# One query tile turned two k-steps later, an output projection that begins with its high parts, and late splits of the second half, in a two-layer decoder step

## The chip, the cores and the metric

The kernel runs on one core of a Trainium2 chip. The metric is the device time of one execution in microseconds (us), the median of several runs; lower is better. The core has a matrix engine (PE; its weight loads are listed apart, as PEld), a vector engine (DVE), a scalar engine (ACT), a general engine (POOL) and a synchronising engine (SP) that here mostly issues transfers (DMAs).

## The reference

One inference step of a decoder with two layers. Layer 0 is a state-space mixer (Mamba-2) and a SwiGLU feed-forward; its output gives one shared set of keys and values. Layer 1 is sliding-window attention with grouped heads over those keys and values, then its output projection, then a second SwiGLU; a final RMS norm ends it. 1024 prompt tokens with 16 learned tokens ahead of them, and 8 x 8 sampled tokens, go through the same weights. The change touches layer 1's attention alone, whose core is

```python
hn = _rmsnorm(h, p['attn_norm_g'][i])
q = _rope_partial((hn @ p['w_q'][i]).reshape(b, l, N_HEADS, HEAD_DIM), pos)
mix = _sliding_sink_attention(q, k_all, v_all, pos0, p['attn_sinks'][i]) @ p['w_o'][i]
h = h + mix
```

All of it is float32, with 16 query heads of 64, 4 key/value heads, and 1024 model columns.

## The kernel before, in words

Activations lie with the model columns on the 128 partitions (8 slices, the k-steps) and the tokens along the free dimension, in two halves of 544 columns in the stage looked at here. A float32 product is made of three products of rounded parts, high by high, high by low and low by high (`mm3`, L75 to L78). The high part of an operand is an ACT cast and the low part a DVE subtraction that waits for the cast (`split_copy`, L81 to L83, for activations; `factor`, L1259 to L1265, for weights: L1263 on ACT, L1264 on DVE).

**Queries.** The generator `queries` (L2237) goes over a = 0 and 1 (the first and the second eight heads) and over prompt tiles i = 1 to 8: eight k-steps of `mm3` give a tile of 128 tokens by 512 query columns. At the last k-step `put_q` scales it on ACT (L2192) and rotates it on POOL (four L2007, then L2008 and L2009) into a tile `qr`. The tile waits in the list `turned`, and during the next tile's k-steps, at k = 5, `turn_queries` transposes it on PE (L2234, four of 128x128) and DVE copies it to QT (L2235). So there are 16 such turns, the last one by itself at the end. For the second heads the weights are split anew: ACT casts (L2028) and DVE subtractions (L2029).

**Attention.** Between these steps `mix` puts the steps of 16 units (`PromptUnit`: tile i, heads a): scores on PE (L2303) with mask and maximum on DVE (L2309), softmax (DVE L2318, L2319, L2327, L2328; ACT exponentials L2326; POOL L2329), and two units later the transposes of the weights (PE L2342, ACT copy L2344, DVE copy L2349) and the values (PE L2360, L2364; copies L2367) into u.O. The last two units run beside the output projection.

**Output projection.** `split` casts and subtracts a unit's u.O into OH[e] and OL[e], the parts of half e (units of tiles 1 to 4 belong to half 0, of tiles 5 to 8 to half 1; a = 0 fills k-steps 0 to 3 and a = 1 fills 4 to 7); the sampled tokens fill the first 32 columns (`split_sampled`). `output_early` (L2472) then makes half 0: for each m of 8 column slices, and each of two chunks c of 272 columns, 24 matmuls into one PSUM tile, the sum with the residual on DVE (L2488), its square on ACT (L2465), and at c = 1 a store to memory that ACT issues (L2491). It yields after every second k-step, and `mix(att, early, 2, 5)` puts steps of the last two units there. `output_tile` (L2496) makes half 1 with k outermost (48 matmuls per m), beside `scale_early`, which turns the squares of half 0 into the norm's scale (PE L1190, DVE L1195 and L1196, POOL L92, DVE L1210, PE L1211, ACT L1212) and applies it to half 0 as loaded back from memory (DVE L1414, L1408, L1415).

**What sets the order.** PE's order here is the program's (`in_order`, L1113); the other engines' is a scheduler's, with priorities (`tc.high_priority`). SP loads, in its own order, each m's slice of w_o in four pieces of 128 KB (L2605) into a ring `ws` of six, the residual rows (L2479), and back from memory the halves hN1 and hN0, two slices m at a time (L2645). The factors `wo` lie in a ring of 12, which is three m.

Of the kernel before, what the change touches and what calls it, by code (L numbers as in the profile page):

```python
# [21 lines left out]
KD = 8  # L22
# [33 lines left out]
EARLY = 14  # L56
# [18 lines left out]
def mm3(nc, out, wH, wL, xH, xL, start, stop):  # L75
    nc.tensor.matmul(out, wH, xH, start=start, stop=False)  # L76
    nc.tensor.matmul(out, wH, xL, start=False, stop=False)  # L77
    nc.tensor.matmul(out, wL, xH, start=False, stop=stop)  # L78


def split_copy(nc, H, L, src):  # L81
    nc.scalar.copy(H, src)
    nc.vector.tensor_tensor(L, src, H.bitcast(F32), ALU.subtract)  # L83
# [1029 lines left out]
def in_order(tc, instructions, engine):  # L1113

    last = None
    for i in instructions:
        if i.engine == engine.engine:
            if last is not None:
                info = mybir.DependencyInfo(mybir.DependencyClass.NoSync, mybir.DependencyReason.DATA)
                tc.add_manual_dep(i, last.name, info, reason="order")  # L1120
            last = i
# [24 lines left out]
def together(a, b):  # L1146

    for _ in a:
        next(b, END)
        yield  # L1150
    for _ in b:
        pass
# [115 lines left out]
class Units:  # L1268
# [22 lines left out]
    def rows(self, w0, w1):  # L1291


        def load(t, w):
            self.nc.sync.dma_start(t[:], w)

        def blocks(r0, r1):
            return {"A11": r0[:, :512], "A21": r0[:, 512:], "A12": r1[:, :512], "A22": r1[:, 512:]}

        self.queue.append([load, (w0, w1), blocks, None])  # L1300
# [824 lines left out]
def qkv(tc, K, A, ap, fp, ps, O, I, pre):  # L2125


    nc = tc.nc
    cs = lambda i, n: A.rope[:n, 8 * i : 8 * i + 8]
    sn = lambda i, n: A.rope[:n, 72 + 8 * i : 80 + 8 * i]  # L2130
    size = lambda i: 128 if i else NX
    start = lambda i: NX + 128 * (i - 1) if i else 0
# [12 lines left out]
    def rows_mm(i, w):  # L2145

        n = size(i)
        acc = ps.rows()
        for k in range(KD):
            mm3(nc, acc[:n, :], *pre.operand(k, i), w[k][0][:], w[k][1][:], k == 0, k == KD - 1)  # L2150
            yield acc
# [36 lines left out]
    def put_q(i, acc, dst):  # L2188
        n = dst.shape[0]
        v = lambda t, p: t.rearrange(p, e=2, q=4)  # L2190
        for e in range(2):
            nc.scalar.mul(v(dst, "p (q e d) -> p e q d")[:, e], v(acc[:n, :], "p (e q d) -> p e q d")[:, e], r8[i][:n])  # L2192
        rope_rows(nc, fp, dst, n, 8, cs(i, n), sn(i, n), nc.gpsimd)

    late = []
# [14 lines left out]
    with tc.high_priority(PRIO):  # L2210
        w = [pre.weights.split(k, raw[0][k], K.g_attn) for k in range(KD)]
# [17 lines left out]
    def turn_queries(i, a, rows):  # L2229

        pq = ps.turned()
        pv = pq[:].rearrange("p (j s h c) -> p j h s c", j=2, s=2, h=2)
        for q in range(4):
            nc.tensor.transpose(pv[:, q // 2, q % 2], rows[:, 128 * q : 128 * q + 128], K.ident)  # L2234
        nc.vector.tensor_copy(A.QT[:, i - 1, a], pq[:])  # L2235

    def queries(w):  # L2237
        turned = [sampled_turned]
        for a in range(2):
            for i in range(1, 9):  # L2240
                for k, acc in enumerate(rows_mm(i, w)):
                    if k == 5 and turned:
                        turned.pop(0)()
                    if k == KD - 1:
                        dst = fp.tile([128, 512], F32, name="qr", tag="row", bufs=2)[:]
                        put_q(i, acc, dst)
                        turned.append(lambda i=i, a=a, dst=dst: turn_queries(i, a, dst))
                    if k % 2:
                        yield
            if a == 0:  # L2250
                with tc.high_priority(PRIO):
                    w = [pre.weights.split(k, raw[1][k], K.g_attn) for k in range(KD)]
        A.last_turn = turned.pop(0)

    return queries(w)


# [202 lines left out]
def output_square(nc, K, F, sqh, hv, e, m, o=0):  # L2460

    n = hv.shape[1]
    d = K.tot[:, 544 * e + o : 544 * e + o + n]
    t = d if m == 0 else sqh()[:, :n]
    nc.scalar.activation(t, hv, AF.Square)  # L2465
    if m == KD - 1 and e:
        F.last_square = t
    elif m:
        (nc.vector if e or m == KD - 1 else nc.gpsimd).tensor_tensor(d, d, t, ALU.add)


def output_early(nc, K, F, sqh, rows, oH, oL):  # L2472


    for m in range(KD):
        u = F.units.get(1)
        w = [u.factor(nm) for nm in ("lo", "hi")]
        x = F.units.raw()[:, :544]
        nc.sync.dma_start(x, F.saved[0][:, m])  # L2479
        F.units.load(2)  # L2480
        for c in range(2):
            acc = rows()
            cs = slice(272 * c, 272 * c + 272)
            for k in range(KD):
                wH, wL = (t[:, 128 * (k % 4) : 128 * (k % 4) + 128] for t in w[k // 4])
                mm3(nc, acc[:, :272], wH, wL, oH[:, k, cs], oL[:, k, cs], k == 0, k == KD - 1)
                if k == KD - 1:
                    nc.vector.tensor_tensor(x[:, cs], x[:, cs], acc[:, :272], ALU.add)  # L2488
                    output_square(nc, K, F, sqh, x[:, cs], 0, m, 272 * c)
                    if c:  # L2490
                        nc.scalar.dma_start(F.saved[0][:, m], x)  # L2491
                if k % 2:
                    yield
# [19 lines left out]
def attention(tc, K, I, O, pre):  # L2513


    nc = tc.nc
    A, F = Ctx(), pre.F
    tp = lambda **kw: tc.tile_pool(reuse_waits="tile", **kw)
    traced = nc.cur_bb.bb.instructions
    with ExitStack() as outer:  # L2520
        outer.enter_context(F.stack.pop_all())
        with ExitStack() as inner:
# [32 lines left out]
            with tp(name="qf", bufs=1) as fp:  # L2555
# [9 lines left out]
                units = [PromptUnit(K, A, i, a, sp, ps) for a in range(2) for i in range(8)]  # L2565

                def prompt(first, last, done=lambda u: None):

                    n = len(units)
                    for x in range(first, last):  # L2570
                        if x >= 2:
                            units[x - 2].turn(0)
                        if x < n:
                            units[x].scores(0)
                        yield
                        if x >= 2:
                            units[x - 2].turn(1)
                        if x < n:
                            units[x].scores(1)
                            units[x].softmax()  # L2580
                        yield
                        if x >= 2:
                            units[x - 2].values()
                            done(units[x - 2])
                            yield
# [6 lines left out]
                att = together(prompt(0, EARLY), sample)  # L2592
# [25 lines left out]
            def split(u):  # L2618

                e, fs, o = u.i // 4, slice(4 * u.a, 4 * u.a + 4), 32 + 128 * (u.i % 4)  # L2620
                split_copy(nc, OH[e][:, fs, o : o + 128], OL[e][:, fs, o : o + 128], u.O)

            def split_sampled(e, o, a, b):
                split_copy(nc, OH[e][:, :, o : o + b - a], OL[e][:, :, o : o + b - a], A.OS[:, :, a:b])

            with tc.high_priority(PRIO):
                split_sampled(0, 0, 40, 64)
                split_sampled(0, 24, 32, 40)
                for i in range(4):
                    split(units[i])  # L2630
                    split(units[8 + i])
            split_sampled(1, 0, 0, 32)
            for i in range(4, 8):
                split(units[i])
            early = output_early(nc, K, F, sqh, ps.rows, OH[0], OL[0])
            att = prompt(EARLY, len(units) + 2, split)
            for _ in range(AHEAD):
                next(att)
            A.last_turn()
# [9 lines left out]
        for m in range(KD):  # L2649
            at = len(traced)  # L2650
# [16 lines left out]
def trunk(tc, I, O):  # L2667
    K = Ctx()
    K.nc = tc.nc
    with tc.tile_pool(name="const", bufs=1) as cp:  # L2670
        build_consts(tc, K, cp, I)
        K.cp = cp
        K.h = [cp.tile([128, KD, 592], F32, name="hA", tag="h0")]
        K.tot = cp.tile([128, 1104], F32, name="tot")
        with tc.tile_pool(name="w1", bufs=1) as wp:
            Q = Weights(tc.nc, wp)
            m = Mamba(tc, K, cp, Q, I, O)
            m.run()
        pre = Prepare(tc, K, I)
        m.F.run(pre)  # L2680
        attention(tc, K, I, O, pre)
# [124 lines left out]
```

## Time and profile before

| | us |
|---|---|
| median of 3 runs | 2751.78 |
| lowest and highest | 2743.92, 2752.15 |
| the profiled execution | 2752.1 |
| its span on the core | 2750.3 |
| PE busy in the span | 2690.7 (98%) |
| DVE, ACT, POOL busy | 1937.3, 1180.9, 499.1 |

The span is the time from the first to the last instruction in the trace; all times inside it are counted from its start. The queries and the attention of layer 1 lie at about 1700 to 1940, the early output projection at 1905 to 1971, the second half's at 1971 to 2020. PE is busy nearly all the time, so the stretches in which it stands are what a change of order can win.

### The profile page before, as it was taken

What the parts mean: (1) busy time and instruction counts of PE and PEld (TensorE: products, weight loads), DVE (VectorE), ACT (ScalarE), POOL (GpSimd) and SP (SyncE); (2) the same over time, 40 slices, a digit from 0 to 9 for tenths busy, and PEclk for the clock granted to TensorE, in tenths of its full rate; (3) what the DMA queues carried; (4) which work ended last, traced back from release to release, by engine and by line L of the source; (5) the groups of instructions that cost most, each with busy time, mean ns of one, the idle gap of its engine ahead of it and who ended that gap; (6) DMA issues with size and microseconds to landing.
All of it is one profiled execution on the core that took longest, in us unless ns stands there. A gap on an engine that the chain in (4) does not pass through costs nothing. (4 is left out here: it accounts for less than half of the span.)

```text
span 2750.3 us, 49923 instructions
## 1 busy us (share of the span) xinstructions
PE 2690.7 (98%) x19545; PEld 2491.6 (91%) x19545; DVE 1937.3 (70%) x3354; ACT 1180.9 (43%) x2480; POOL 499.1 (18%) x707
## 2 busy tenths in 40 slices
PE   8999999999999999999999999999999999999998
PEld 7888898987888899999999997676999999999998
DVE  6878666576564787777778881556488777777887
ACT  5766544266441543333342143556344333334123
POOL 3566544025322000000000002433200000000001
PEclk9999999999999999999999999999999999999999
DMA  8876766665554344444487652011724444447764
GB/s 292 281 240 221 261 233 241 235 225 194 191 187 157 111 160 154 146 136 163 145 300 277 228 193 82 27 48 32 214 68 150 160 144 136 159 144 284 273 231 165
DMA packets 266347, 501.00 MB, mean 182 GB/s; under 512 B 23792, under 2 KB 144240, under 8 KB 266112
## 3 DMA queue, kind: packets, MB, share of 16 engines
q1 hardware_dynamic: 262368, 491.10, 52.2%
q10 hardware_dynamic: 3744, 6.72, 0.7%
q8 instruction: 154, 2.52, 0.4%
q14 instruction: 81, 0.66, 0.1%
HBM read 322.44 MB, written 175.30 MB: 181 GB/s over the span
## 5 line engine op out<-in xcount | busy, mean ns | idle before, releaser
L1263 ACT CAST wo<-ws 128x512 fp32r<-128x512 f32 x424 | 261.8, 621 | 493.9 <-PE wacc L1625 218.4
L1625 PE MATMUL dacc<-bo,wo 128*128 128x276 f32 (+1 forms) x1232 | 356.1, 289 | 0.0
L1624 PE MATMUL dacc<-bo,wo 128*128 128x276 f32 (+1 forms) x1232 | 355.0, 288 | 0.0
L1626 PE MATMUL dacc<-bo,wo 128*128 128x276 f32 (+1 forms) x1232 | 354.9, 288 | 0.0
L1264 DVE TENSOR_TENSOR wo<-ws,wo 128x512 fp32r<-128x512 f32 x424 | 290.2, 689 | 50.3 <-ACT wo L1263 46.7
L76 PE MATMUL acc<-uH,wH 128*128 128x336 f32 (+2 forms) x808 | 266.2, 329 | 7.0 <-DVE th L850 5.6
L78 PE MATMUL acc<-uH,wL 128*128 128x336 f32 (+2 forms) x808 | 266.8, 330 | 1.3 <-POOL wL L150 1.2
L77 PE MATMUL acc<-uL,wH 128*128 128x336 f32 (+2 forms) x808 | 265.9, 329 | 0.0
L1624 PEld LDWEIGHTS dacc<-bo,wo 128*128 128x128 f32 x1232 | 232.8, 189 | 0.4 <-ACT sumX L1813 0.4
L1626 PEld LDWEIGHTS dacc<-bo,wo 128*128 128x128 f32 x1232 | 231.8, 188 | 0.0
L1625 PEld LDWEIGHTS dacc<-bo,wo 128*128 128x128 f32 x1232 | 231.8, 188 | 0.0
L76 PEld LDWEIGHTS acc<-uH,wH 128*128 128x128 f32 x808 | 154.0, 191 | 22.0 <-DVE th L850 5.8
L668 DVE SCALAR_TENSOR_TENSOR cc<-raw,vectors_sb,cc 128x616 f32<-128x616 f32 (+1 forms) x144 | 138.5, 966 | 42.2 <-ACT cc L666 40.3
L78 PEld LDWEIGHTS acc<-uH,wL 128*128 128x128 f32 x808 | 153.6, 190 | 13.6 <-issue 3.7
L77 PEld LDWEIGHTS acc<-uL,wH 128*128 128x128 f32 x808 | 153.7, 190 | 11.3 <-issue 2.7
L76 PE MATMUL acc<-yH,wH 128*128 128x336 f32 (+1 forms) x360 | 122.8, 341 | 8.3 <-DVE hA L930 2.6
L2543 POOL MEMSET mask<- 128x64 f32 x1 | 0.2, 152 | 706.1 <-PE dacc L1626 706.1
L78 PE MATMUL acc<-yH,wL 128*128 128x336 f32 (+1 forms) x360 | 120.8, 335 | 0.6 <-DMA wL<-kept 0.6
L77 PE MATMUL acc<-yL,wH 128*128 128x336 f32 (+1 forms) x360 | 120.5, 335 | 0.7 <-DVE yL L83 0.7
L1263 ACT CAST wo<-sum 128x512 fp32r<-128x512 f32 x62 | 38.5, 621 | 174.9 <-PE wacc L1625 130.7
L1624 PE MATMUL wacc<-N4H,wo 128*128 128x276 f32 (+1 forms) x352 | 102.2, 290 | 3.7 <-DVE hN L1644 2.0
L1801 DVE TENSOR_TENSOR hN<-hN,dacc 128x552 f32<-128x552 f32 (+1 forms) x128 | 91.7, 722 | 19.1 <-PE dacc L1626 18.6
(576 smaller groups left out, 8425.0 us busy)
## 6 DMA issues: line engine op xcount, KB each, us to landing
kept<-wH SPq DMA_DIRECT2D x56, 512.0 KB, 2.8
kept<-wL SPq DMA_DIRECT2D x56, 512.0 KB, 3.1
ws<-ffn_w_gate SPq DMA_DIRECT2D x44, 512.0 KB, 4.2
ws<-ffn_w_up SPq DMA_DIRECT2D x44, 512.0 KB, 5.1
ws<-ffn_w_down SPq DMA_DIRECT2D x44, 512.0 KB, 5.9
ws<-ssm_w_in SPq DMA_DIRECT2D x40, 512.0 KB, 5.3
wH<-kept SPq DMA_DIRECT2D x38, 512.0 KB, 3.6
wL<-kept SPq DMA_DIRECT2D x38, 512.0 KB, 4.5
```

What stands on the lines that cost most here:

```text
L76: nc.tensor.matmul(out, wH, xH, start=start, stop=False)
L77: nc.tensor.matmul(out, wH, xL, start=False, stop=False)
L78: nc.tensor.matmul(out, wL, xH, start=False, stop=stop)
L668: nc.vector.scalar_tensor_tensor(o, raw[:, k : k + n], w(k), o, ALU.mult, ALU.add)
L1263: nc.scalar.copy(H, src)
L1264: (low or nc.vector).tensor_tensor(L, src, H.bitcast(F32), ALU.subtract)
L1624: nc.tensor.matmul(out, wH, xH, start=start, stop=False, skip_group_check=True)
L1625: nc.tensor.matmul(out, wH, xL, start=False, stop=False, skip_group_check=True)
L1626: nc.tensor.matmul(out, wL, xH, start=False, stop=stop, skip_group_check=True)
L1801: add = lambda d, s: nc.vector.tensor_tensor(d, d, s, ALU.add)
L2543: nc.gpsimd.memset(A.mask0[:, :NS], NEG)
```

## The change

It has three parts. The turn of the first heads' last tile, which happens during the second heads' first tile, is made at k = 7 and not at k = 5. The first chunk of the output projection makes all its products with OH first (16 matmuls) and then those with OL (8), all before its first yield. The splits of half 0 run in the order of units 0, 1, 8, 9, 2, 3, 10, 11 (before: 0, 8, 1, 9, 2, 10, 3, 11), and those of half 1 are all put behind the values of the last unit, chained in that order on ACT and on DVE.

```diff
-                    if k == 5 and turned:
+                    if k == (KD - 1 if a and i == 1 else 5) and turned:
                         turned.pop(0)()
...
+            if m == 0 and c == 0:
+                for late in range(2):
+                    for k in range(KD):
+                        wH, wL = (t[:, 128 * (k % 4) : 128 * (k % 4) + 128] for t in w[k // 4])
+                        if late:
+                            nc.tensor.matmul(acc[:, :272], wH, oL[:, k, cs], start=False, stop=k == KD - 1)
+                        else:
+                            nc.tensor.matmul(acc[:, :272], wH, oH[:, k, cs], start=k == 0, stop=False)
+                            nc.tensor.matmul(acc[:, :272], wL, oH[:, k, cs], start=False, stop=False)
             for k in range(KD):
-                wH, wL = (t[:, 128 * (k % 4) : 128 * (k % 4) + 128] for t in w[k // 4])
-                mm3(nc, acc[:, :272], wH, wL, oH[:, k, cs], oL[:, k, cs], k == 0, k == KD - 1)
+                if m or c:
+                    wH, wL = (t[:, 128 * (k % 4) : 128 * (k % 4) + 128] for t in w[k // 4])
+                    mm3(nc, acc[:, :272], wH, wL, oH[:, k, cs], oL[:, k, cs], k == 0, k == KD - 1)
...
-                for i in range(4):
-                    split(units[i])
-                    split(units[8 + i])
-            split_sampled(1, 0, 0, 32)
-            for i in range(4, 8):
-                split(units[i])
+                for i in (0, 2):
+                    for a in range(2):
+                        split(units[8 * a + i])
+                        split(units[8 * a + i + 1])
+            def split_later(u):
+                if u is units[-1]:
+                    at = len(traced)
+                    split_sampled(1, 0, 0, 32)
+                    for x in range(4, 8):
+                        split(units[x])
+                        split(units[8 + x])
+                    for eng in (nc.vector, nc.scalar):
+                        last = [i for i in traced[at - 40 : at] if i.engine == eng.engine][-1]
+                        in_order(tc, [last] + traced[at:], eng)
+
-            att = prompt(EARLY, len(units) + 2, split)
+            att = prompt(EARLY, len(units) + 2, split_later)
```

The order of PE around the moved turn, before (-) and now (+); L2342 and L2360 are steps of the attention units, L77 and L78 the query tile's products:

```order
 L77 MATMUL pP<-rwL,u_17269 128x512
 L78 MATMUL pP<-rwH,u_17270 128x512
-L2234 MATMUL pT<-cmask_sb,qr 128x2x64 x4
 L2342 MATMUL pT<-cmask_sb,work 128x128
 L2342 MATMUL pO<-cmask_sb,work 128x128
...
 L77 MATMUL pP<-rwL,u_17269 128x512
 L78 MATMUL pP<-rwH,u_17270 128x512
+L2234 MATMUL pT<-cmask_sb,qr 128x2x64 x4
 L2360 MATMUL pO<-work,V 64x256 x4
 L2364 MATMUL pO<-work,V 64x256 x4
```

One turn, the eighth of 16, has moved behind six more products of its neighbour tile and one step of attention.

The order of DVE from the projection's first subtractions on (OL_20182 is half 0, OL_20183 half 1; L2498 is L2488 of before):

```order
 L83 TENSOR_TENSOR OL_20182<-QT,OH_20180 128x4x128 x6
-L83 TENSOR_TENSOR OL_20183<-OS,OH_20181 128x8x32
-L83 TENSOR_TENSOR OL_20183<-QT,OH_20181 128x4x128 x4
-L1264 TENSOR_TENSOR wo<-ws,wo 128x512
-L2327 TENSOR_TENSOR work<-work 128x4
-L2309 ISA work<-pS,am_sb,sink 128x192
...
+L83 TENSOR_TENSOR OL_20183<-OS,OH_20181 128x8x32
+L2498 TENSOR_TENSOR ws<-ws,pP 128x272
+L83 TENSOR_TENSOR OL_20183<-QT,OH_20181 128x4x128 x5
+L2498 TENSOR_TENSOR ws<-ws,pP 128x272
+L83 TENSOR_TENSOR OL_20183<-QT,OH_20181 128x4x128 x3
+L1264 TENSOR_TENSOR wo<-ws,wo 128x512
```

Five subtractions of half 1 have left the place ahead of the score step L2309, and all nine now stand together after the last unit.

The order of DVE around the scale of half 0, in the second half's projection (hN_21010 is half 0 as loaded back, hN_21011 half 1; L2518 is L2508 of before):

```order
-L2508 TENSOR_TENSOR hN_21011<-hN_21011,wacc 128x544
-L1264 TENSOR_TENSOR wo<-ws,wo 128x512
+L2518 TENSOR_TENSOR hN_21011<-hN_21011,wacc 128x544
 L1414 TENSOR_TENSOR sum<-hN_21010,tot 128x256
 L1408 SCALAR_TENSOR_TENSOR hN_21010<-hN_21010,vectors_sb,tot 128x512 x5
 L1415 TENSOR_TENSOR hN_21010<-sum,vectors_sb 128x8x32
 L1408 SCALAR_TENSOR_TENSOR hN_21010<-hN_21010,vectors_sb,tot 128x512 x3
-L1264 TENSOR_TENSOR wo<-ws,wo 128x512
-L1245 TENSOR_TENSOR sum<-ws 128x512
-L2508 TENSOR_TENSOR hN_21011<-hN_21011,wacc 128x544
+L1264 TENSOR_TENSOR wo<-ws,wo 128x512 x2
+L2518 TENSOR_TENSOR hN_21011<-hN_21011,wacc 128x544
```

A weight's subtraction that stood ahead of the group L1414 to L1408 stands behind it now; it is that of k-steps 4 to 7 of m = 3, made from ws_21054. On SP the pieces of ws_21054 have moved too (before, then now; L2615 is L2605 and L2664 is L2645 of before):

```order
-L2605 DMA ws_21054<-w_o 64x4x128 x3
-L2605 DMA ws_21119<-w_o 64x4x128 x4
-L2645 DMA hN0_21010<-res0_9633 128x2x544
-L2605 DMA ws_21054<-w_o 64x4x128
-L2605 DMA ws_21219<-w_o 64x4x128 x4
...
+L2615 DMA ws_21359<-w_o 64x4x128 x4
 L1284 DMA ws_21364<-ffn_w_gate 128x8x128
-L2645 DMA hN0_21010<-res0_9633 128x2x544
+L2664 DMA hN0_21010<-res0_9633 128x2x544 x2
+L2615 DMA ws_21054<-w_o 64x4x128 x2
```

Two of the four pieces now come after everything else of w_o and after both last loads of hN0.

## Rows read from the trace of the kernel before

**Rows 1.** The list of waits of PE, 1500 to 2100: us, times, longest.

```profile
PE pT L2234 <- POOL qr L2009: 3.7, 2, 2.9
PE pP L77 <- DVE OL L83: 2.2, 1, 2.2
PE ps L1211 <- DVE tot L1210: 1.9, 1, 1.9
```

**Rows 2.** The timeline of PE, the seventh and the eighth turn: start, us, [idle before].

```profile
1784.12 0.66 PE L2234 MATMUL pT<-cmask_sb,qr 128*128 128x128 f32 x4 [2.92 <-POOL qr L2009]
...
1799.97 0.60 PE L2234 MATMUL pT<-cmask_sb,qr 128*128 128x128 f32 x4
```

**Rows 3.** The timeline of POOL, the rotations of those two tiles.

```profile
1778.85 4.55 POOL L2007 TENSOR_TENSOR rt<-qr,rope_sb 128x64 f32<-128x64 f32 x4
...
1792.86 1.14 POOL L2007 TENSOR_TENSOR rt<-qr,rope_sb 128x64 f32<-128x64 f32 x4 [8.80 <-ACT qr L2192]
```

**Rows 4.** The timeline of DVE beside the slow rotation.

```profile
1779.93 2.73 DVE L2029 SCALAR_TENSOR_TENSOR rwL<-QT,vectors_sb,rwH 128x512 fp32r<-128x512 f32 x4
```

**Rows 5.** Busy time by stretch: span, then PE, PEld, DVE, ACT, POOL, clock, DMA share, GB/s.

```profile
1786.00:1788.00 2.00, 2.00 (x12) 1.50 (x12) 1.10 (x3) 0.59 (x1) 0.00 (x0) 0.50 0.01 4
...
1964.00:1978.00 14.00, 14.00 (x114) 13.84 (x114) 4.86 (x9) 4.00 (x8) 1.54 (x2) 1.00 0.94 233
...
1983.00:1986.00 3.00, 3.00 (x15) 3.00 (x15) 1.26 (x3) 1.32 (x3) 0.00 (x0) 0.50 1.01 204
```

**Rows 6.** The timeline of PE, the early output projection.

```profile
1905.47 0.39 PE L76 MATMUL pP<-OH,wo 128*128 128x272 f32 x1
1908.07 0.39 PE L77 MATMUL pP<-OL,wo 128*128 128x272 f32 x1 [2.21 <-DVE OL L83]
...
1910.31 0.27 PE L2342 MATMUL pT<-cmask_sb,work 128*128 128x128 f32 x1
...
1911.06 0.92 PE L2303 MATMUL pS<-KT,QT 64*128 64x192 f32 x8
...
1915.18 1.59 PE L2303 MATMUL pS<-KT,QT 64*128 64x192 f32 x8 [0.85 <-DVE work L2309]
...
1928.44 0.65 PE L2360 MATMUL pO<-work,V 128*64 128x256 f32 x2 [0.81 <-ACT work L2344]
```

**Rows 7.** The timeline of DVE, subtractions of half 0, and the scores.

```profile
1907.34 3.70 DVE L83 TENSOR_TENSOR OL<-QT,OH 128x512 fp32r<-128x512 f32 x6
...
1914.36 0.42 DVE L2309 CUSTOM_DVE_ANT_0 work<-pS,am_sb,sink 128x192 f32<-128x192 f32 x1
```

**Rows 8.** The timeline of ACT, casts of half 0 and of half 1.

```profile
1902.40 4.26 ACT L82 CAST OH<-QT 128x512 fp32r<-128x512 f32 x8
...
1927.30 0.60 ACT L82 CAST OH<-QT 128x512 fp32r<-128x512 f32 x1
```

**Rows 9.** The timeline of PE in the second half's projection.

```profile
1971.45 0.37 PE L76 MATMUL wacc<-OH,wo 128*128 128x272 f32 x1
...
1982.30 2.41 PE L1211 MATMUL ps<-tot,cmask_sb 32*128 32x32 f32 x10 [1.92 <-DVE tot L1210]
...
1997.84 0.29 PE L76 MATMUL wacc<-OH,wo 128*128 128x272 f32 x1
```

**Rows 10.** The timeline of ACT there: the last store of half 0 and the casts behind it.

```profile
1978.87 0.33 ACTq L2491 DMA_DIRECT2D res<-ws  x1
1979.24 1.14 ACT L1263 CAST wo<-ws 128x512 fp32r<-128x512 f32 x2 [7.12 <-DMA ws<-w_o]
```

**Rows 11.** The timeline of SP there: pieces of w_o and the last load of hN0.

```profile
1971.17 11.93 SPq L2605 DMA_DIRECT2D ws<-w_o  x13
...
1983.80 0.58 SPq L2645 DMA_DIRECT2D hN<-res  x1
```

**Rows 12.** The timeline of DVE there: the scale of half 0 and the subtraction behind.

```profile
1989.97 0.43 DVE L1414 TENSOR_TENSOR sum<-hN,tot 128x256 f32<-128x256 f32 x1 [5.71 <-ACT wo L1263]
...
1995.94 0.69 DVE L1264 TENSOR_TENSOR wo<-ws,wo 128x512 fp32r<-128x512 f32 x1
```

## The prediction, as put on record before the changed kernel ran

> **What bounds the kernel.** PE works almost without a break, so I looked first at the list of PE's waits in this stage: three entries matter, a turn that waits for a rotated query tile, a product that waits for a low part, and the scale of half 0 that waits for DVE [rows 1]. Then I followed each on the timelines: which turn it is [rows 2], what held the engine that it waits for [rows 3, 4], and the same for the output projection [rows 6 to 8] and the second half's projection [rows 9 to 12]. The sum is made against the profiled execution, 2752.1 us (span 2750.3), 0.3 us above the median of the runs shown, 2751.78.
>
> **The moved turn.** The long wait, 2.92 us, is the turn at 1784.12 [rows 2]. That is the seventh of the 16. The change moves the eighth, at 1799.97, which has no idle time before it: its rotation began at 1792.86 and its four L2007 took 1.14 us [rows 3]. For the seventh tile the same four took 4.55 us [rows 3], while DVE split the second heads' weights back to back, 2.73 us for four from 1779.93 [rows 4]. So the wait belongs to that meeting of POOL and DVE, and the diff moves neither. The Trainium skill, "GPSIMD Engine Reference", Specifications, says that GpSimd shares its SBUF interface with VectorE and contends with DVE instructions that read two SBUF operands. The subtractions at L2029 read two, and the trace agrees: 4.55 us beside them, 1.14 us without. By that rule the wait stays at the seventh turn, whatever is done with the eighth. A reading by the wait list alone would count the 2.92 us as won, and with it about 1 us of the 2 us in which the granted clock was 0.50 behind it, the lower of the two levels, 1.2 of 2.4 GHz [rows 5]. I take 0 for this edit: the six products and the attention step that change places with the turn are the same work. Its bounds are 0 and -3.9 us.
>
> **The first chunk and the split order.** Before, the first product with OL waits 2.21 us, and 18 products are through at 1910.31 [rows 6], so that one product takes (1910.31 - 1908.07) / 18 = 0.125 us. Now 16 products with OH come first: 1905.47 + 0.1 (the first is longer) + 16 x 0.125 = 1907.57. Their casts, of units 0, 1, 8 and 9, are four of a row of eight that began at 1902.40 and took 4.26 / 8 = 0.53 us each [rows 8], done by 1904.6, and cost no wait. The eight products with OL begin at 1907.57. The first four need units 0 and 1, subtracted before 1907.34. The others need the two next subtractions, 3.70 / 6 = 0.62 us each from 1907.34 [rows 7], done at 1908.57, so PE still waits about 0.5 us at 1908.07. All 24 are through at about 1909.2. Before, 24 would have been through at 1910.31 + 6 x 0.125 = 1911.06: gain **1.9 us**.
>
> The next step depends on the late splits too. The second group of score products began at 1915.18 after 0.85 us of waiting for DVE, whose score step began at 1914.36 [rows 6, 7], behind five subtractions of half 1 that the change takes from there. Now DVE is through with half 0 at 1911.04 [rows 7]; one weight's subtraction (0.69, as in rows 12) and the sum of chunk 0 (0.4, taken as a score step's duration) bring the scores to 1912.1, and two of them (2 x 0.42) release PE at 1912.95. PE would be ready at 1909.2 + 0.75 (the transposes, 1910.31 to 1911.06) + 0.85 + 0.75 (six products) + 0.75 = 1912.3, so 0.65 us of the wait stays, and the gain stands at 1915.18 - 1912.95 = **2.2 us**. At 1928.44 the values waited 0.81 us for an ACT copy behind a cast of half 1, 0.60 us at 1927.30, which is gone [rows 6, 8]: I take 0.8, between 0.4 (the exponentials ahead of it set the time) and 1.0. Together **-3.0 us**, bounds -2.0 and -3.6.
>
> **What the late splits cost.** Nine casts (about 4.7 us by rows 8) and nine subtractions (5.6 us by rows 7) now stand in one piece behind the last unit's values, near 1940. PE needs half 1's parts only from 1971.45 [rows 9], 30 us later, so they cost PE nothing directly. Without that cover they would cost 5.6 us. Queued behind them are the chunk sums that free PE's PSUM tiles (five subtractions, 3.1 us, against the 3.0 us of a chunk of 24 products; bound 0 to +0.5), the weights' subtractions, and with these the release of raw tiles for SP's loads. The factors lie three m ahead, some 18 us, which covers 5.6.
>
> **The scale of half 0.** PE waited 1.92 us at 1982.30 [rows 9], and about 1.5 us more went with the half clock behind it (0.50 over 3 us [rows 5]). The chain: ACT's store of the last slice went out at 1978.87, and two weight casts and their subtractions, ahead of the scale on DVE, had to wait for it [rows 10]. That slice's products ended before 1971.45 [rows 9], so the store was held some 7 us by its transfer queue. There it shares a semaphore with a w_o piece issued late by SP; the new build pairs it with an earlier piece, ahead of the hN0 loads. I take the whole **-3.4 us**, bounds 0 and -3.4.
>
> **The new wait.** In return two of the four pieces for k-steps 4 to 7 of m = 3 come last on SP, after both hN0 loads, and their subtraction stands behind the eight L1408 of half 0's scale on DVE. In the trace before, that place on DVE is 1995.94 + 0.69 = 1996.6 [rows 12], held by the last hN0 load, issued at 1983.80 after 13 pieces in 11.93 us [rows 11]. PE reaches these k-steps at 1997.84 [rows 9], now 6.4 us earlier: 1991.4. The loads follow PE's progress, since PE frees the factors, and PE leads by 3.0 us before the scale; so the factor is there at 1993.6 and PE waits 2.2 us. Bounds: 0 (two pieces fewer stand ahead of the loads, at 0.92 us each, and the rest of the lead reaches them) and +5.2 (the loads do not move at all). I take **+2.1 us**.
>
> Sum: 0 - 3.0 - 3.4 + 2.1 = -4.3; 2752.1 - 4.3 = **2747.8 us**, 0.16%. Its bounds are -7.0 (2745.1) and, with the scale's wait still there, -2.0 (2750.1). No stage behind moves on PE except by this shift.
>
> **Rivals.** *A, all given back.* From 1964 to 1978 the DMA engines were busy 0.94 of the time at 233 GB/s [rows 5]. If the transfers, not PE, set when hN0 and the last pieces land, PE waits 5.2 us at m = 3, with about 1.5 us of half clock behind: -6.4 + 6.7 = +0.3, **2752.4 us**. For it speaks the 0.94; against it that the loads wait on tiles that PE releases. The Trainium skill, "DMA: Bandwidth & Descriptors", Issuing engines are not separate DMA queues, says that transfers issued by several engines end on the same 16 DMA engines and interleave. By that rule an earlier store on ACT's queue buys no room, which is A; no row here tells the two apart.
>
> *B, the turn counts.* If the slow rotation in the new build meets DVE at the eighth tile, or the seventh turn no longer waits, -3.9 comes on top: 2743.9, and with no wait at m = 3 2741.8. Rows 3 and 4 speak against it, since the weights' splits keep their place.
>
> *C, slower.* The nine subtractions delay the raw tiles by their 5.6 us, and a transfer stream at 0.94 doesn't catch up. The factor of m = 3 is then ready at 1996.6 + 5.6 - 3.0 = 1999.2 against PE's 1991.4: 7.8 us of waiting and 1.5 of clock against -6.4 gives +2.9, **2755.0 us**; a second such wait for the feed-forward's first weights, behind the same pieces, 2760.6. It decides if the late splits take more than the three m of factors hide.
>
> **Chances.** Forecast 0.62; A 0.18; B 0.10; C 0.10. A measurement of this kernel can tell about 0.3%, 8.3 us, from no change. Faster by more needs under 2743.5: most of B and a little of the forecast's better end, 0.12. Slower by more needs over 2760.1: the worse half of C, 0.04. The rest, 0.84, is within. The range takes in the forecast's bounds, A, the better part of B and C's first price: 2742.0 to 2755.5.
>
> **What would show it.** Right: the turn at about 1784 still waits 2.9 us; no product waits over 0.8 us for OL; the second score group waits about 0.6 us; L1211 waits under 0.3 us, with the last store issued near 1970; and one wait of about 2 us at the second half of m = 3 on a weight's subtraction. Wrong: a wait of 5 us there (A), a turn without its wait (B), or several PE waits on weights after 1945 (C).

## The result, and the profile after

| | before | changed |
|---|---|---|
| median, us | 2748.53 | 2744.64 |
| lowest and highest, us | 2743.92, 2753.8 | 2738.8, 2749.37 |
| runs | 22 | 22 |
| ratio, 95% interval | | 0.9981, [0.9974, 0.9988] |
| profiled execution, its span, us | 2752.1, 2750.3 | 2741.82, 2740.0 |

The ratio is 5.2 us of 2748.5, between 3.3 and 7.1: a gain, smaller than the 0.3% beyond which the prediction spoke of faster. The two profiled executions differ by 10.3 us, which is more, because stretches that the change doesn't touch differ too. So I cut the stage out of each trace at four marks on PE: an attention step just ahead of the seventh turn (L2389, at 1777.78 before and 1772.34 after), the last turn (L2234, 1903.28 and 1897.86), and the two scales (L1211, 1982.30 and 1971.40, then 2036.42 and 2023.96). The marks on the timelines of PE, as far as no other rows show them, first before, then changed:

```profile
1777.78 0.63 PE L2389 MATMUL pT<-cmask_sb,work 128*64 128x128 f32 x4 [0.50 <-ACT work L2420]
...
1903.28 0.65 PE L2234 MATMUL pT<-cmask_sb,qr 128*128 128x128 f32 x4 [0.74 <-POOL qr L2009]
...
2036.42 1.49 PE L1211 MATMUL ps<-tot,cmask_sb 32*128 32x32 f32 x10
```

```profile
1772.34 0.62 PE L2389 MATMUL pT<-cmask_sb,work 128*64 128x128 f32 x4 [0.50 <-ACT work L2420]
...
1897.86 0.66 PE L2234 MATMUL pT<-cmask_sb,qr 128*128 128x128 f32 x4 [0.74 <-POOL qr L2009]
...
2023.96 1.49 PE L1211 MATMUL ps<-tot,cmask_sb 32*128 32x32 f32 x10
```

| us from mark to mark | turns and attention | early projection, to the first L1211 | to the second L1211 | sum |
|---|---|---|---|---|
| before | 125.50 | 79.02 | 54.12 | 258.64 |
| changed | 125.52 | 73.54 | 52.56 | 251.62 |

Up to the first mark the changed kernel was 5.4 us ahead by chance of its run (e1 below, the same program up to there, reaches that mark at 1778.87); in the stage it won 7.0 us, and 2.2 were lost behind it, 1.5 of them in one place (last section). The list of PE's waits in the changed kernel, 1500 to 2100, against [rows 1]:

```profile
PE pT L2234 <- POOL qr L2009: 3.7, 2, 2.9
...
PE pP L2489 <- DVE OL L83: 0.4, 1, 0.4
PE pO L2342 <- DVE QT L2367: 0.4, 1, 0.4
...
PE pS L2303 <- DVE work L2309: 0.2, 1, 0.2
```

The turn's wait is there unchanged. The wait for OL has fallen from 2.2 to 0.4 us, that of the scores from 0.85 to 0.2, the one for the values' ACT copy is gone, and L1211 waits no more; a small wait of the transposes (L2342, 0.4) is new. The timeline of PE, for [rows 2], [rows 6] and [rows 9]:

```profile
1778.68 1.11 PE L2234 MATMUL pT<-cmask_sb,qr 128*128 128x128 f32 x4 [2.92 <-POOL qr L2009]
...
1798.06 0.60 PE L2234 MATMUL pT<-cmask_sb,qr 128*128 128x128 f32 x4
...
1900.05 0.39 PE L2491 MATMUL pP<-OH,wo 128*128 128x272 f32 x1
...
1902.16 0.67 PE L2489 MATMUL pP<-OL,wo 128*128 128x272 f32 x4
1903.25 0.77 PE L2489 MATMUL pP<-OL,wo 128*128 128x272 f32 x4 [0.42 <-DVE OL L83]
1903.86 0.27 PE L2342 MATMUL pT<-cmask_sb,work 128*128 128x128 f32 x1
...
1907.36 1.59 PE L2303 MATMUL pS<-KT,QT 64*128 64x192 f32 x8 [0.23 <-DVE work L2309]
...
1962.54 0.37 PE L76 MATMUL wacc<-OH,wo 128*128 128x272 f32 x1
...
1971.40 1.49 PE L1211 MATMUL ps<-tot,cmask_sb 32*128 32x32 f32 x10
...
1985.38 0.29 PE L76 MATMUL wacc<-OH,wo 128*128 128x272 f32 x1
```

The chunk took 1903.86 - 1900.05 = 3.81 us for 24 products; before, 24 would have taken 1911.06 - 1905.47 = 5.59. The last row is the first product of k-step 4 of m = 3, where the new wait was forecast: there is none. The same place on the other engines, for [rows 10] to [rows 12], first the last store on ACT, then SP, then DVE:

```profile
1962.81 0.33 ACTq L2501 DMA_DIRECT2D res<-ws  x1
```

```profile
1950.60 16.81 SPq L2615 DMA_DIRECT2D ws<-w_o  x22
1967.52 0.54 SPq L1284 DMA_DIRECT2D ws<-ffn_w_gate  x1
1968.11 1.09 SPq L2664 DMA_DIRECT2D hN<-res  x2
1969.24 1.47 SPq L2615 DMA_DIRECT2D ws<-w_o  x2
```

```profile
1975.65 0.43 DVE L1414 TENSOR_TENSOR sum<-hN,tot 128x256 f32<-128x256 f32 x1 [5.42 <-DMA hN<-res]
...
1981.63 1.29 DVE L1264 TENSOR_TENSOR wo<-ws,wo 128x512 fp32r<-128x512 f32 x2
```

The store goes out with the last square of half 0; the last two loads of hN0 go out between 1968.11 and 1969.20, and the factor for the late k-steps is ready by 1982.9, 2.5 us before PE needs it.

### The profile page after: what moved, and what is told of

It reads as the page before. It is cut to its first block, busy times and chain, and to the rows that moved or that the text cites. A ratio compares the mean times of both kernels' runs of the same rounds, so it can differ in the third digit from the quotient of the medians.

```text
span 2740.0 us, 49927 instructions
## 1 busy us (share of the span) xinstructions
PE 2687.6 (98%) x19545; PEld 2489.8 (91%) x19545; DVE 1936.3 (71%) x3354; ACT 1181.0 (43%) x2480; POOL 499.5 (18%) x707
## 4 chain that ended last, share of the span: by engine, by line
PE 86%; DVE 7%; ACT 3%; DMA 3%; issue 1%; POOL 0%; SPq 0%; POOLq 0%; DVEq 0%; ACTq 0%
PE wacc L1624 10%; PE wacc L1626 10%; PE wacc L1625 10%; PE acc L76 6%; PE acc L78 6%; PE acc L77 6%; PE dacc L1624 6%; PE dacc L1625 6%; PE dacc L1626 6%; PE pP L76 2%; PE pP L77 2%; PE pP L78 2%; DVE cc L668 1%; DMA E<-acsd 1%; PE ps L758 1%
## 5 line engine op out<-in xcount | busy, mean ns | idle before, releaser
L1264 DVE TENSOR_TENSOR wo<-ws,wo 128x512 fp32r<-128x512 f32 x424 | 291.8, 693 | 42.3 <-ACT wo L1263 36.3
L78 PE MATMUL acc<-uH,wL 128*128 128x336 f32 (+2 forms) x808 | 266.3, 330 | 1.3 <-POOL wL L150 1.2
L77 PE MATMUL acc<-uL,wH 128*128 128x336 f32 (+2 forms) x808 | 265.6, 329 | 0.0
L78 PEld LDWEIGHTS acc<-uH,wL 128*128 128x128 f32 x808 | 153.3, 190 | 13.7 <-issue 3.7
L77 PEld LDWEIGHTS acc<-uL,wH 128*128 128x128 f32 x808 | 153.5, 190 | 11.3 <-issue 2.7
L78 PE MATMUL acc<-yH,wL 128*128 128x336 f32 (+1 forms) x360 | 120.0, 333 | 1.1 <-DMA wL<-kept 1.1
L77 PE MATMUL acc<-yL,wH 128*128 128x336 f32 (+1 forms) x360 | 119.6, 332 | 0.7 <-DVE yL L83 0.7
```

The lines of the kernel that those rows point to most:

```text
L1264: (low or nc.vector).tensor_tensor(L, src, H.bitcast(F32), ALU.subtract)
```

## The experiments

All times are compared with runs of the kernel before on the same chip. The table gives each ratio, and the stage from the profile as above.

| kernel | ratio, 95% interval | turns and attention | to the first L1211 | to the second | sum |
|---|---|---|---|---|---|
| changed | 0.9981 [0.9974, 0.9988] | 125.52 | 73.54 | 52.56 | 251.62 |
| e1, eighth turn put back | 0.9990 [0.9981, 0.9998] | 125.50 | 73.54 | 52.57 | 251.61 |
| e2, seventh turn moved | 0.9955 [0.9943, 0.9968] | 120.97 | 73.55 | 52.56 | 247.08 |
| e3, first chunk alone | 1.0007 [0.9997, 1.0017] | 128.34 | 79.41 | 54.25 | 262.00 |
| e4, late splits alone | 0.9998 [0.9989, 1.0007] | 125.50 | 77.70 | 54.28 | 257.48 |
| e5, seventh rotation on DVE | 0.9960 [0.9947, 0.9974] | 121.25 | 73.53 | 55.62 | 250.40 |
| e6, before, store on POOL | 0.9995 [0.9985, 1.0005] | 125.49 | 77.03 | 52.56 | 255.08 |
| e7, before, seventh turn alone | 0.9974 [0.9963, 0.9986] | 120.94 | 79.50 | 54.17 | 254.61 |

**e1, the moved turn taken back.**

```diff
-                    if k == (KD - 1 if a and i == 1 else 5) and turned:
+                    if k == 5 and turned:
```

> The change without its moved turn: the eighth turn is back at k = 5, the rest is kept. Theory: the moved turn buys nothing, since the turn that waits is the seventh. This run then has the same waits as the changed kernel: 2.9 us at the seventh turn, none at the eighth, 0.4 us for OL, no wait at L1211, and its time is within 1 us of the changed kernel's (about 5 us under the kernel before). Rival: the moved turn counts, and this run loses up to 3.9 us against the changed kernel, a wait standing at the eighth turn.

The stage is the same to 0.01 us and the waits are the same. By time e1 lies 0.0009 (2.5 us) above the changed kernel, where within 1 us was expected; their intervals overlap. The moved turn buys nothing in the trace.

**e2, the condition set one tile earlier.**

```diff
-                    if k == (KD - 1 if a and i == 1 else 5) and turned:
+                    if k == (KD - 1 if a == 0 and i == 8 else 5) and turned:
```

> The changed kernel with the condition set on the tile before: the seventh turn (first heads, during tile 8) is made at k = 7, the eighth at k = 5 again. Theory: the rotation that meets the weights' splits is ready some 2.9 us late, six more products and an attention step cover it, so the wait at the seventh turn falls from 2.9 to under 0.3 us, the half clock behind it goes too, and PE is 3 to 4 us ahead of the changed kernel from there on (about 9 us under the kernel before). Rival: what stands next in line waits in its place (the scores of that tile, or the next rotation), and less than 1 us is won.

The stage is 4.5 us shorter than the changed kernel's, all of it in the first column, and the ratio of 0.9955 lies, with its interval, wholly below that of the changed kernel. It is the lowest ratio of all kernels run here, though the intervals of e5 and e7 overlap it. Its timelines of POOL and PE:

```profile
1772.70 5.53 POOL L2007 TENSOR_TENSOR rt<-qr,rope_sb 128x64 f32<-128x64 f32 x4
...
1778.59 0.32 POOL L2009 TENSOR_TENSOR qr<-rt,rt 128x64 f32<-128x64 f32 x1
```

```profile
1779.84 0.60 PE L2234 MATMUL pT<-cmask_sb,qr 128*128 128x128 f32 x4
```

The rotation is no faster (5.53 us against 4.54 in the changed kernel); the tile is ready at 1778.9, and PE comes for it at 1779.84.

**e3, the first chunk and the order of half 0's splits alone**, on the kernel before (the hunks of the change at `output_early` and at the first splits; half 1's splits and the turn as before).

> The kernel before with the new first chunk and the new split order of half 0 alone; the splits of half 1 stay where they were, the turn too. Theory: the chunk is through 1.8 us earlier (wait for OL 0.4 to 0.6 instead of 2.2), but the second group of scores then waits for DVE, which still has the five subtractions of half 1 ahead: about 2.4 us instead of 0.85, so that hardly anything is won by then (0.3 us); the wait at L1211 stays at 1.9 us, since SP's order stays. In all 0 to -1 us against the kernel before. Rival: the chunk's gain stands by itself: -1.8 us, the second wait not growing.

```profile
PE pS L2303 <- DVE work L2309: 2.9, 1, 2.9
PE pO L2342 <- DVE QT L2367: 1.0, 1, 1.0
...
PE pP L2489 <- DVE OL L83: 0.4, 1, 0.4
```

As expected, the chunk's wait fell to 0.4 and the scores' wait rose to 2.9 us (list of PE's waits, 1900 to 1990). It also cost half clock behind it, seen in the busy time of these two stretches, where the clock is the number behind POOL's:

```profile
1917.00:1920.00 3.00, 2.29 (x9) 1.67 (x9) 3.00 (x15) 2.05 (x5) 0.09 (x1) 0.55 0.00 0
1920.00:1924.00 4.00, 4.00 (x19) 4.00 (x18) 4.00 (x11) 0.62 (x1) 3.61 (x2) 0.50 0.34 101
```

The kernel before had 1.00 in 1918 to 1922, behind its shorter wait. L1211 did not wait, against the expectation. SP's order is the old one, yet the store was issued 73.2 us behind the last turn (1978.73 - 1905.54) and not 75.6 (1978.87 - 1903.28): the piece of w_o that has the same semaphore landed 5.1 us after its issue, and before it took 7.7. PE also came to L1211 2.3 us later (79.41, against 79.02 less the wait of 1.92), which is more than that wait. The 2.8 us more in the first column are a longer half clock behind the seventh turn, in code that is the same (0.50 still in 1790 to 1794, where the kernel before had 1.00). By time e3 is at 1.0007, with 1 inside its interval.

**e4, the late splits alone**, on the kernel before (`split_later` and its call; the chunk, the order of half 0's splits and the turn as before).

> The kernel before with the splits of half 1 late alone: the first chunk, the order of half 0's splits and the turn stay as they were. Theory: the wait of 2.2 us for OL stays; the second scores' wait (0.85 us) and the values' wait (0.8 us) go, 1.5 us together; SP's order changes with the late splits, so the wait of 1.9 us at L1211 and its 1.5 us of half clock go as well. In all about -5 us against the kernel before, some 2 us less than the changed kernel wins in this stage. Rival: L1211 is freed by PE being earlier, not by SP's order; its wait then stays and the gain is 1.5 us.

L1211 lost its wait as expected, and not by the rival: PE is no earlier there (77.70 us behind the last turn, against 79.02 - 1.92 = 77.10 before), while SP's last two loads of hN0 now go out together, as in the changed kernel:

```profile
1977.01 1.09 SPq L2653 DMA_DIRECT2D hN<-res  x2
```

But the time did not fall: 0.9998, where -5 us would be 0.9982. Two terms failed. The scores still waited, 0.47 and 1.29 us, with half clock behind (0.50 in 1918 to 1920). The timelines of DVE and POOL show why:

```profile
1911.49 1.95 DVE L1264 TENSOR_TENSOR wo<-ws,wo 128x512 fp32r<-128x512 f32 x1
1913.36 0.41 DVE L2309 CUSTOM_DVE_ANT_0 work<-pS,am_sb,sink 128x192 f32<-128x192 f32 x1
...
1914.04 1.28 DVE L1264 TENSOR_TENSOR wo<-ws,wo 128x512 fp32r<-128x512 f32 x1
```

```profile
1911.42 3.34 POOL L2329 TENSOR_TENSOR work<-work 128x768 f32<-128x768 f32 x2 [8.83 <-ACT work L2344]
```

The scheduler filled the freed place with weights' subtractions, and these ran beside POOL's normalisation, at 1.95 and 1.28 us instead of 0.69. The second ends at 1915.32, 0.56 us behind the end of POOL's two (1914.76), as if it had stood until then and run afterwards. And the clock fell again ahead of the second scale, with no wait of PE: 0.50 in 2031 to 2033, some 3 us behind a run of products of one column (L1190). The changed kernel has the same run, and 1.00 behind it (2020 to 2022); in e3 the clock fell there as well (0.55 in 2035 to 2037).

```profile
2031.00:2033.00 2.00, 2.00 (x11) 2.00 (x10) 0.36 (x2) 1.13 (x2) 0.00 (x0) 0.50 0.00 0
```

So neither half of the second edit wins by itself by time; together they take 5.5 us off the middle column, 1.9 of it the wait at L1211.

**e5, the seventh rotation on DVE**, all turns at k = 5.

```diff
-        rope_rows(nc, fp, dst, n, 8, cs(i, n), sn(i, n), nc.gpsimd)
+        rope_rows(nc, fp, dst, n, 8, cs(i, n), sn(i, n), eng or nc.gpsimd)
...
-                        put_q(i, acc, dst)
+                        put_q(i, acc, dst, nc.vector if a == 0 and i == 7 else None)
```

> The changed kernel with all turns at k = 5, but tile 7 of the first heads rotated on DVE and not on POOL (six small operations ahead of the scores' step there). Theory: the seventh turn waits because POOL's rotation is held while DVE's weight splits run; on DVE the tile is ready before these splits begin, so the wait of 2.9 us and the half clock behind it go without any turn being moved: 3.5 to 4.5 us won against the changed kernel from there on, as with the seventh turn moved. Rival: the tile is late for another reason (the scale on ACT, DVE's own queue), and the wait stays above 1.5 us.

```profile
1776.41 0.60 PE L2234 MATMUL pT<-cmask_sb,qr 128*128 128x128 f32 x4
```

The seventh turn has no wait, without having been moved, and the first column falls by 4.3 us. A new wait in the third column (1.46 us at L1190, at 2010.48, for DVE's sum of squares) and a half clock (0.50 in 2018 to 2021) give 3.1 back in this profile. The half clock comes some 7 us behind that wait, at the place where e3 and e4 had one without a wait, so that it need not be the wait's.

**e6, one store moved to another queue**, on the kernel before.

```diff
-                        nc.scalar.dma_start(F.saved[0][:, m], x)
+                        (nc.gpsimd if m == KD - 1 else nc.scalar).dma_start(F.saved[0][:, m], x)
```

> The kernel before, with one thing changed: the last store of half 0 is issued by POOL and not by ACT, so it no longer stands ahead of two weight casts in ACT's queue, nor waits for the w_o piece whose semaphore it shared. Nothing else moves. Theory: the two casts run near 1972 and not 1979, the scale of half 0 follows 5 us earlier, the wait of 1.9 us at L1211 goes with its half clock, and the time falls by 3.4 us, without the rest of the change. Rival: the scale is held by the raw tile's landing (the cast's recorded wait is for a transfer), so the wait at L1211 stays above 1 us. The chunk's wait (2.2 us) and the second scores' wait (0.85 us) stay in both.

```profile
1969.56 0.62 ACT L1263 CAST wo<-ws 128x512 fp32r<-128x512 f32 x1 [2.49 <-DMA ws<-w_o]
```

```profile
1975.26 1.49 PE L1211 MATMUL ps<-tot,cmask_sb 32*128 32x32 f32 x10
```

```profile
1964.62 9.89 SPq L2605 DMA_DIRECT2D ws<-w_o  x13
...
1975.21 0.88 SPq L2645 DMA_DIRECT2D hN<-res  x1
```

The cast runs 5.7 us before L1211 where it ran 3.1 before it [rows 9, 10]; L1211 does not wait, and the stage is 3.6 us shorter. But this execution does not show that the moved store did it. The piece whose semaphore the store had shared, the first of the 13 in the SP row, was issued at 1964.62 and landed 5.7 us later, at 1970.3, where it took 7.7 us before. An estimate from that: on ACT's queue, too, the store could have gone at 1970.3, and L1211 would have been ready 3.4 us later, as before (1982.30 - 1978.87), at 1973.7, ahead of PE's 1975.26. The chunk's 2.2 us stayed. By time, 0.9995 with an interval of 0.9985 to 1.0005 holds both -3.4 us (0.9988) and nothing.

**e7, the seventh turn alone**, on the kernel before (the diff of e2).

> The kernel before with the seventh turn made at k = 7, and nothing else. Theory: the wait of 2.9 us at that turn and the half clock behind it go, 4.5 us up to the last turn as in the run on the changed kernel; the chunk's wait of 2.2 us, the second scores' wait and SP's order stay. In all about -4.5 us against the kernel before. Rival: the gain is given back later, at the first chunk or at L1211, where the engines that PE waits for are not earlier: -1 us or less.

```profile
1975.64 2.29 PE L1211 MATMUL ps<-tot,cmask_sb 32*128 32x32 f32 x10 [1.89 <-DVE tot L1210]
```

The first column falls by 4.6 us and L1211's wait stays. In all 4.0 us in the stage, 0.9974 by time. One condition in one line of the kernel before does about as much as the whole change.

## Why the prediction was right, and where it was not

**The moved turn: 0, measured 0.** The seventh turn waits 2.92 us as before, and e1 shows in the trace that the eighth one's place is worth nothing. The reason holds too: e5, with the rotation off POOL, has no wait there. For the rule of the Trainium skill, "GPSIMD Engine Reference", Specifications, on the shared SBUF interface, the trace agrees, with more numbers: four L2007 take 4.54 to 5.53 us beside the subtractions L2029, and in e4 DVE's L1264 takes 1.95 beside POOL's L2329. That the two engines hold each other up is shown; that the shared interface is the cause was not tried by itself.

**The chunk: 1.9 forecast, 1.8 measured** (5.59 - 3.81), with 0.42 us of wait for OL where 0.5 was forecast. **To the second scores: 2.2 forecast, 2.4 measured** (1915.18 - 5.42 - 1907.36, by the shift of 5.42 us up to the last turn). **With the values: 3.0 forecast, 3.5 measured**; the wait at L2360 went, and a new one of 0.37 us at L2342 took little of it (shift -8.91 by the second half's first product, 1971.45 and 1962.54). e3 and e4 add what the prediction only half said: the chunk's gain exists only because DVE's five subtractions leave, and their leaving pays only with the chunk's new order.

**The late splits: 0, measured 0** on PE: nine subtractions ran between 1932 and 1938, and no product waited between 1945 and 2050.

**The scale: -3.4 forecast, -3.55 measured** in the profiles (shift -8.91 ahead of it, -12.46 behind). The trace bears the mechanism out. Before, the piece of w_o issued at 1971.17 [rows 11] landed 7.7 us later, at 1978.85, and the store, which waits on that piece's semaphore, went out at 1978.87. In the changed kernel the store's semaphore is that of a piece issued at 1957.01, which landed 4.3 us later, so the store was not held; and e4, with that order on SP and PE no earlier, has no wait at L1211 either. But the old order does not make the wait by itself: of the four profiles that have it, the kernel before and e7 wait, e3 and e6 do not. In e3 PE came later by more than the wait, and in e6 the piece was issued and landed sooner. Of the five with the new order none waits. So the full 3.4 is an upper end for the median, and what this term is worth by time no run shows; e6, which was to show it, does not.

**The new wait: +2.1 forecast, 0 measured.** This is the step that failed: "The loads follow PE's progress, since PE frees the factors, and PE leads by 3.0 us before the scale". Counted from the last turn, SP had issued the last load of hN0 by 1984.38 - 1903.28 = 81.1 us before and by 1969.20 - 1897.86 = 71.3 us after, 9.8 earlier and not 3.0, where PE led by 3.5 (8.91 - 5.42). What had held SP was not PE alone. Before, pieces of w_o waited for loads of hN to land, on semaphores that they shared (the list of SP's waits, 1900 to 1990, kernel before):

```profile
SPq L2605 <- DMA hN<-res: 6.7, 3, 3.4
```

In the changed order the third load of hN0 no longer stands among the pieces; that wait is absent from the list, and 22 pieces go out in 16.81 us, 0.76 each, where 13 took 11.93, or 0.92 each [rows 11]. That the order counts, e4 shows: its last load is out 75.5 us behind its last turn (1978.10 - 1902.65), 5.6 earlier than before, with PE 0.6 later. But part of such a gain is the execution's: e6, in the old order, is 3.2 earlier than the kernel before (1976.09 - 1898.23 = 77.9). How the 9.8 divide between the order, PE's lead and chance stays open. The factor still hung on the last load, as the prediction said (L1414 waited 5.42 us for hN), but it was ready 2.5 us early, inside the bound of 0 that the prediction gave.

**The sum** was -4.3 us; the stage won 7.0 in the profile, and the runs say 5.2 (3.3 to 7.1). That -4.3 lies so near to 5.2 is in part luck: a loss of 2.1 that did not come stands against a profile that won 1.8 more than the runs did. Of the signs that the prediction named for being right all came but the last, the wait at m = 3, and the second scores waited 0.23 us where about 0.6 was named. And its 2747.8 us lies 3.2 above the measured 2744.64 because the execution that it counted from, 2752.1, lies 3.6 above the median of the 22 runs of the kernel before.

Rival A (transfers set the pace) fell: PE had no wait at m = 3, and the loads went out 9.8 us earlier while the DMA engines were as busy as before, 0.93 of the time in the stretch that matches 1964 to 1978 of [rows 5]:

```profile
1955.00:1969.00 14.00, 14.00 (x114) 13.84 (x113) 6.22 (x15) 3.99 (x8) 2.16 (x5) 1.00 0.93 222
```

With it fell what hung on the Trainium skill's "DMA: Bandwidth & Descriptors", Issuing engines are not separate DMA queues: no run here shows that rule right or wrong. Rival B (the turn counts) fell with e1, C (the late splits delay the weights) since PE has no wait between 1945 and 2050.

## What to carry to other kernels

Before moving work away from a wait, count which instance of it waits: the list gave one line for 16 turns, only the timeline said that it was the seventh, and the same edit one tile earlier (e2) won 4.5 us more. Two edits on one chain of engines are to be priced together, since each alone only hands the wait to the next engine in line (e3, e4). And a transfer's issue time is to be read from what its queue waits for, landings on shared semaphores included, not from the progress of the engine that uses it. A wait that comes in some executions only (L1211's, in two of four profiles of the old order) is not to be credited to an edit by one profile without it: look up in both profiles when the transfer behind it landed (e6).

## What the runs showed of the hardware that was not expected

The price of a wait on PE is not its length alone: the clock may fall to half behind it, and whether it does differs between the profiles of kernels whose code is the same there. Behind the seventh turn's 2.9 us it fell in all six kernels that have it, and cost 2.8 us more in e3 than in the others. Behind the chunk's 2.2 us it stayed at 1.00 before (1908 to 1912) and fell in e7 (0.51 in 1901 to 1904). A wait of 2.0 to 2.1 us in the feed-forward (PE for DVE's hN at L1644) left it at full speed before and cost 1.5 us more in the changed kernel, in these stretches behind the wait, before and changed:

```profile
2139.00:2141.00 2.00, 2.00 (x19) 2.00 (x18) 1.25 (x2) 0.71 (x2) 0.00 (x0) 1.00 0.99 383
```

```profile
2127.00:2129.00 2.00, 2.00 (x11) 2.00 (x10) 0.99 (x2) 0.42 (x1) 0.00 (x0) 0.50 0.99 379
```

19 products against 11 in 2 us, and the changed kernel's lead falls there from 12.3 to 10.8 us. Those are 1.5 of the 2.2 us lost behind the stage, no part of the change; of nine kernels two show it there. Ahead of the stage the first mark lies between 1771.63 and 1778.87 in the nine profiles, with the same program. So single executions differ ahead of the stage by up to 7.2 us, as much as the whole change won in it, and the edits were read from mark to mark.
